# Moving the second layer's split input and merged branches two elements further in SBUF

## The chip, the cores and the metric

The kernel runs on one core of one Trainium2 chip. The metric is the device time of one launch in microseconds (us); lower is better. Times without a profile are medians over runs. A profile is one more execution, recorded by the hardware profiler.

## The reference

A two-layer encoder over 272 tokens (16 learned tokens in front of 256 real ones, numbered 0 to 271 below), with 2048 channels, in float32. Cut to what matters here:

```python
for i in range(2):
    h = rmsnorm(x, norm_mix[i])
    q, k, v, f, ga, gf = split(h @ w_in[i])                 # one projection of the normed input
    a = attention(rope(rmsnorm(q)), rope(rmsnorm(k)), v) @ w_attn_br[i]
    s = fft2(f).real @ w_four[i]
    merged = sigmoid(ga + b) * a + sigmoid(gf + b) * s
    x = x + merged @ w_out[i]
    up = rmsnorm(x, norm_ffn[i]) @ w_up[i]                  # 2048 -> 2 * 5632
    g = conv3(up[:, :5632]) * w + b                         # over tokens t-1, t, t+1
    x = x + (silu(g) * up[:, 5632:]) @ w_down[i]
return x[16:]                                               # the 16 learned tokens are dropped
```

Only tokens 16 to 271 are returned. So in the second layer most of the work is done for tokens 16 to 271 alone, or, where the convolution needs the token before, for tokens 14 to 271, which is 258 columns.

## The kernel before

Everything is stored with channels on the 128 partitions and tokens along a partition. Each float32 matrix product is made from numbers split in two parts of reduced precision, a high part H and a low part L, and three products are summed in PSUM: weight H by input H, weight H by input L, weight L by input H.

The weights stream from HBM in chunks of 512 KB (128 partitions by 4 KB) into four buffers `raw`, ScalarE casts a chunk to its high part `wh` (L242), VectorE subtracts to make the low part `wl` (L245), and TensorE uses the two as stationary operands. A planner writes out the whole sequence of chunks before the first instruction; loads and splits run two chunks ahead of the products, and the order in which TensorE takes its groups is written out by hand.

The function `group` is where nearly all products are made: for a pair of 128-channel outputs it goes over all chunks, and for each 128-channel slice of the input issues the three products, each with its own load of stationary weights:

```python
a, b = x
nc.tensor.matmul(o, h[:, c, sl], a, start=kt == 0, stop=False)         # L314
nc.tensor.matmul(o, h[:, c, sl], b, start=False, stop=False)           # L315
nc.tensor.matmul(o, lo[:, c, sl], a, start=False, stop=kt == nk - 1)   # L316
```

The input that streams through the array is one row of `T` = 272 tokens of a split tensor, 1,088 bytes of a partition, or a part of that row from token `lo` on. In the first layer `lo` is 0; in the second it is 14 for the queries, the gates, the branch and output projections and the gate half of the FFN, and `lo2` is 16 for the value half of the FFN.

The tensors that the change touches:

- `xHL` (L388 and the line below it) holds the normed input of the projections, as 16 slices of two rows each, H and L. It is written by `norm_split` (L458 and L459), in the first layer for the mixing part, at the end of that layer's output projections for its FFN, in the first layer's last `w_down` groups for the second layer, and at the end of the second layer's output projections for its FFN. It is read by all projections `f`, `k`, `v`, `q`, `ga`, `gf` and by both FFN halves `ug` and `uv`. In the second layer `uv` reads H and L of a slice with one product of two rows of 256 tokens (L310, 512 columns) and H again with the low weights (L311, 256 columns).
- `mHf` and `mLf`, in pool slots of `AHn` and `ALn` elements, hold the merged branches, 8 rows of 272 tokens each, written by ScalarE and VectorE after each attention branch group `a`, and read by the output projections `o`. The same slots serve for other tensors earlier in the layer: the attention weights `PH` and `PL`, the folded input and the channel transforms.
- The attention output `qH`, `qL`, read by the groups `a`, is not touched by the change.

The last 12 blocks of the second layer's FFN and the products of its `w_down` work the other way around: there the activations (`tH`, `tL`, `opnd`) are stationary and the split weights stream as 512 or 256 columns (L1291, L1356).

Addresses: a pool gives each tile a place that is a multiple of 32 bytes in the partition. In the built program `xHL` starts at byte 33,920, which is 530 times 64, and a row of 272 tokens is 17 times 64 bytes. So in the program before, every row of `xHL` starts on a multiple of 64 bytes, token 14 lies 56 bytes behind such a multiple, and token 16 lies on one. The second layer's `mH` and `mL` start 32 bytes behind a multiple of 64, and their token 14 lies 24 bytes behind one.

Of the kernel before, what the change touches and what calls it, by code (L numbers as in the profile page):

```python
# [10 lines left out]
F32 = mybir.dt.float32  # L11
F32R = mybir.dt.float32r
AF = mybir.ActivationFunctionType
# [3 lines left out]
P = 128  # L17
# [3 lines left out]
T = NM + SEQ  # L21
DEPTH = 2
KT = D // P
# [11 lines left out]
FF_SPLIT = (24, 20)  # L35
# [97 lines left out]
def encoder_kernel(ctx, tc, xT, params, consts, bmat, cfold, csign, w_fl, w_f64c, w_in, w_abr, w_four, w_f64, w_out, w_up, w_down, w_dn, w_dt, out):  # L133
    nc = tc.nc
# [48 lines left out]
    t, done = 0, 0  # L183
# [174 lines left out]
    def first_groups(pss):  # L358
        assert order[st["grp"]][0] == (0, "f01")
        st["grp"] += 1  # L360
        ps = [psum.tile([P, 512], F32, tag="mm", name=f"ps_f01_{m}") for m in range(2 * MG)]
        pss += [ps[:MG], ps[MG:]]
        for kt in range(KT // CW * 2 * CW):
            q, j, c = kt // (2 * CW), kt // CW % 2, kt % CW
            k = CW * q + c
            if c == 0:
                if kt == 0:
                    norm_split(0, P_NM)
                    split_w(0, 0, 1)
                    norm_split(1, P_NM)  # L370
                    split_w(0, 1, 2)
                    norm_split(2, P_NM)
                    split_w(0, 2, 4)
                    norm_split(3, P_NM)
                    st["fetch"] = 1
                h, lo = splits.pop(st["next"])
                st["next"] += 1
            for m in range(MG):
                sl = slice(m * P, (m + 1) * P)
                o = ps[MG * j + m][:, :T]  # L380
                a, b = xH[:, k, :], xL[:, k, :]
                nc.tensor.matmul(o, h[:, c, sl], a, start=k == 0, stop=False)
                nc.tensor.matmul(o, h[:, c, sl], b, start=False, stop=False)
                nc.tensor.matmul(o, lo[:, c, sl], a, start=False, stop=k == KT - 1)
            if j == 1 and CW * (q + 1) + c < KT:
                norm_split(CW * (q + 1) + c, P_NM)
            if c in (0, 2):
                advance(st["next"] + (1 if c == 0 else 2))  # L388
                pump(len(chunks))
            if kt == 0:  # L390
                tc.keep_in_program_order(nc.sync.dma_start(XT[:, 12:16, :], xT[:, 12:16, :]))
                tc.keep_in_program_order(nc.sync.dma_start(cst[:, C_MASK:C_CC], consts[:, C_MASK:C_CC]))
            step()


    XT = per.tile([P, KT, T], F32, name="XT")
    xHL = per.tile([P, KT, 2, T], F32R, name="xHL")
    xH, xL = xHL[:, :, 0, :], xHL[:, :, 1, :]
    prm = per.tile([P, P_N], F32, name="prm")
    cst = per.tile([P, C_N], F32, name="cst")  # L400
    ones = per.tile([P, P], F32, name="ones")
# [53 lines left out]

    def norm_split(m, goff):
        gc = prm[:, goff + m:goff + m + 1]
        nc.scalar.activation(xH[:, m, :], XT[:, m, :], AF.Copy, scale=gc)  # L458
        nc.vector.scalar_tensor_tensor(xL[:, m, :], XT[:, m, :], gc, xH[:, m, :].bitcast(F32),  # L459
                                       op0=ALU.mult, op1=ALU.subtract)  # L460

    def norm_sum(m):
# [75 lines left out]
        nc.vector.tensor_tensor(tok2, tok, tok, op=ALU.mult)  # L538
        holder["tok2"] = tok2

    xr = lambda lo: (lambda kt: (xH[:, kt, lo:T], xL[:, kt, lo:T]))
    slow[1] = weight_sums()

    for l in range(DEPTH):
# [6 lines left out]
        with tc.tile_pool(name=f"mix{l}", bufs=1) as mp:  # L551
            E = mp.tile([P, 4, 2, TH] if last else [P, NG, T], F32, tag="q1b" if last else "q1", name="E")
            e64 = mp.tile([2 * NG, TH], F32, tag="u", name="e64", bufs=2) if last else None
            AHn = 3 * 4 * T
            ALn = 2 * 4 * T
            o1 = []

            def o1_tiles():
# [422 lines left out]
            def attention(kv, rq):  # L981
# [6 lines left out]
                PHf = mp.tile([P, AHn], F32R, tag="aH", name="PH")  # L988
                PLf = mp.tile([P, ALn], F32R, tag="aL", name="PL")
                PH = PHf.rearrange("p (b h t) -> p b h t", b=3, h=4)  # L990
                PL = PLf.rearrange("p (b h t) -> p b h t", b=2, h=4)

                def scores(item):
                    if item is None:
# [124 lines left out]
            for half in range(2):  # L1119
                slow[2] = 0  # L1120
                mH = mL = None
                for kind, i in BRANCH_ORDER[half]:
                    j = i - 4 * half
                    if kind == "ga":
                        tha[i] = gate("ga", i)
                    elif kind == "gf":
                        w64s.append(split_w64(l, i))
                        thf[i] = gate("gf", i)
                    elif kind == "s":
                        def s_evac(m, ps, th=thf[i]):  # L1130
                            e, o = (mp.tile([P, TH], F32, tag=t, name=t) for t in ("se", "so"))
                            for a, p_ in ((e, ps[0]), (o, ps[1])):
                                nc.scalar.copy(a, p_[:, TH:2 * TH])
                                nc.vector.tensor_tensor(a, p_[:, :TH], a, op=ALU.add)
                            sp = mp.tile([P, T], F32, tag="sp", name="sp", bufs=2)
                            nc.vector.tensor_tensor(sp[:, 0:TH], e, o, op=ALU.add)
                            nc.vector.tensor_tensor(sp[:, TH:T], e[:, T - TH:0:-1], o[:, T - TH:0:-1], op=ALU.subtract)
                            t_ = th[:, m, lo:T]
                            nc.vector.scalar_tensor_tensor(t_, t_, 1.0, sp[:, lo:T], op0=ALU.add, op1=ALU.mult)

                        four_group((l, "s", i), fr, x64, w64s.pop(0), s_evac)
                    else:
                        if mH is None:
                            drain()
                            mHf = mp.tile([P, AHn], F32R, tag="aH", name="mH")
                            mLf = mp.tile([P, ALn], F32R, tag="aL", name="mL")
                            mH = mHf[:, :8 * T].rearrange("p (k t) -> p k t", k=8)
                            mL = mLf[:, :8 * T].rearrange("p (k t) -> p k t", k=8)
                        ps = group((l, "a", i), lambda kt: (qH[kt // 4][:, kt % 4, lo:T], qL[kt // 4][:, kt % 4, lo:T]), W)
                        for m in range(MG):  # L1150
                            k = 2 * j + m
                            t_, h_ = tha[i][:, m, lo:T], mH[:, k, lo:T]
                            nc.vector.scalar_tensor_tensor(t_, t_, 1.0, ps[m][:, :W], op0=ALU.add, op1=ALU.mult)
                            nc.vector.tensor_tensor(t_, t_, thf[i][:, m, lo:T], op=ALU.add)
                            nc.scalar.copy(h_, t_)
                            nc.vector.tensor_tensor(mL[:, k, lo:T], t_, h_.bitcast(F32), op=ALU.subtract)
                slow[2] = (18 if last else 24) if last or half else 0
                for mg in range(8):
                    ps = group((l, "o", half, mg), lambda kt: (mH[:, kt, lo:T], mL[:, kt, lo:T]), W)
                    for m in range(MG):  # L1160
                        mt = 2 * mg + m
                        nc.vector.scalar_tensor_tensor(XT[:, mt, lo:T], ps[m][:, :W], 0.5, XT[:, mt, lo:T], op0=ALU.mult, op1=ALU.add)
                        if half == 1:
                            norm_in(mt, P_NF + l * KT)


        with tc.tile_pool(name=f"ffn{l}", bufs=1) as fp:
# [25 lines left out]
            def split_to(h, low, v):  # L1193
                nc.scalar.copy(h, v)
                nc.vector.tensor_tensor(low, v, h.bitcast(F32), op=ALU.subtract)

            k0 = 0
            for c, n in enumerate(() if last else FF_SPLIT):
                gHL = fp.tile([P, FF_SPLIT[0], 2, T], F32R, tag="gHL", name="gHL")
                gH, gL = gHL[:, :, 0, :], gHL[:, :, 1, :]  # L1200
                for i in range(k0 // MG, (k0 + n) // MG):
                    cs = conv_gate(i)
                    ps = group((l, "uv", i), xr(0), T)
                    for m in range(MG):
                        j = 2 * i + m - k0
                        nc.vector.tensor_tensor(cs[m], cs[m], ps[m][:, :T], op=ALU.mult)
                        split_to(gH[:, j], gL[:, j], cs[m])
                for mg in range(8):
                    ps = group((l, "d", c, mg), lambda kt: (gH[:, kt], gL[:, kt]), T)
                    for m in range(MG):  # L1210
                        mt = 2 * mg + m
                        nc.vector.tensor_tensor(XT[:, mt], XT[:, mt], ps[m][:, :T], op=ALU.add)
                        if c == len(FF_SPLIT) - 1:
                            norm_in(mt, P_NM + (l + 1) * KT)
                k0 += n
# [3 lines left out]
            if last:  # L1219
# [92 lines left out]
                for i in range(FT // MG):  # L1312
                    cs = conv_gate(i)
                    if i == 0:
                        for s_ in range(2):
                            nc.vector.tensor_scalar(sgn[:, s_], hold["tok"][:, 1:3], 1.0 - 2 * s_, None, op0=ALU.mult)
                    ps = group((l, "uv", i), lambda kt: (xHL[:, kt, :, lo2:T],), W2)
                    for m in range(MG):
                        j = 2 * i + m
                        cv = cs[m][:, lo2:T]  # L1320
# [111 lines left out]
```

## Time and profile before

| | |
|---|---|
| median of 3 runs | 2552.93 us (2552.89 to 2554.19) |
| the profiled execution's own time | 2552.66 us |
| its span, first to last instruction | 2550.8 us |
| TensorE busy | 2541.1 us, 19184 matmuls |
| weight loads | 2467.0 us |
| VectorE busy | 1775.1 us |
| ScalarE busy | 1270.8 us |
| moved by DMA | 591.45 MB, mean 232 GB/s |

The profile names a group of instructions by its line in the kernel, its engine, its operation, and what it writes and reads (out<-in) with shapes; then come the count, the busy time in us and the mean duration of one in ns, and after the bar the idle time of the engine just before them. A matmul's duration runs until its last column has left the array, so durations of successive matmuls overlap: their sum is more than the time that passes, and differences of durations between shapes show what columns cost.

### The profile page before, as it was taken

The page shows a single profiled execution, that of the slowest core. Times are in us where ns is not written, and L with a number is a line of the kernel's source. Part 1 is how long each engine was busy: PE and PEld are TensorE (multiplying, and loading weights), DVE is VectorE, ACT ScalarE, POOL GpSimd, SP SyncE. Part 2 cuts the span into 40 slices and gives each one's busy share as a digit, 9 for nine tenths or more (in the row PEclk, how much of TensorE's full clock was granted, in tenths as well). Part 3 has the DMA queues.
Part 4 walks back from the last instruction along what each step waited for, and adds up shares of the span by engine and source line. Part 5 has one row for each costly group of instructions (what it writes and reads, how often), then busy time and mean ns, then how long its engine had stood idle before and what let it go on. Part 6 is the DMA issues. An engine that isn't in the chain of part 4 may idle for free.

```text
span 2550.8 us, 47527 instructions
## 1 busy us (share of the span) xinstructions
PE 2541.1 (100%) x19184; PEld 2467.0 (97%) x19184; DVE 1775.1 (70%) x2804; ACT 1270.8 (50%) x1820; POOL 78.4 (3%) x169
## 2 busy tenths in 40 slices
PE   9999999999999999999999999999999999999999
PEld 8999999999999999999999999999999999988887
DVE  7687866776666556666559877666756666788886
ACT  5455434554444334444445555444644444566665
POOL 0000000000000000000000000000000000000000
PEclk9999999999999999999999999999999999999999
DMA  6545555689898988888775546765878555787887
GB/s 237 165 155 160 192 181 180 221 249 298 273 280 286 281 298 275 289 272 281 236 228 193 180 142 194 240 211 193 258 251 253 189 183 187 226 265 262 259 303 247
DMA packets 158731, 591.45 MB, mean 232 GB/s; under 512 B 18080, under 2 KB 23328, under 8 KB 158000
## 3 DMA queue, kind: packets, MB, share of 16 engines
q1 hardware_dynamic: 147344, 519.19, 60.5%
q0 software_dynamic: 9728, 67.11, 10.8%
q8 instruction: 150, 2.46, 0.4%
q10 hardware_dynamic: 1440, 2.13, 0.2%
q14 instruction: 69, 0.57, 0.1%
HBM read 566.70 MB, written 85.98 MB: 256 GB/s over the span
## 4 chain that ended last, share of the span: by engine, by line
PE 98%; DMA 1%; DVE 1%; issue 0%; ACT 0%; SPq 0%; POOL 0%; ACTq 0%
PE ps_ug L315 7%; PE ps_ug L316 7%; PE ps_ug L314 7%; PE ps_uv L310 6%; PE ps_p L1291 6%; PE ps_d L315 3%; PE ps_uv L314 3%; PE ps_uv L315 3%; PE ps_d L314 3%; PE ps_uv L316 3%; PE ps_d L316 3%; PE ps_uv L311 3%; PE ps_t L1356 3%; PE ps_o L315 2%; PE ps_gf L314 2%; PE ps_gf L315 2%
## 5 line engine op out<-in xcount | busy, mean ns | idle before, releaser
L245 DVE TENSOR_TENSOR wl<-raw,wh 128x1024 fp32r<-128x1024 f32 (+1 forms) x901 | 1090.9, 1218 | 640.1 <-ACT wh L242 629.2
L242 ACT CAST wh<-raw 128x1024 fp32r<-128x1024 f32 (+1 forms) x901 | 937.5, 1044 | 968.1 <-PE ps_ug L315 195.1
L315 PE MATMUL ps_ug<-xHL,wh 128*128 128x272 f32 (+1 forms) x1408 | 402.3, 286 | 0.0
L314 PE MATMUL ps_ug<-xHL,wh 128*128 128x272 f32 (+1 forms) x1408 | 402.3, 286 | 0.0
L316 PE MATMUL ps_ug<-xHL,wl 128*128 128x272 f32 (+1 forms) x1408 | 401.5, 285 | 0.0
L314 PEld LDWEIGHTS ps_ug<-xHL,wh 128*128 128x128 f32 x1408 | 265.2, 188 | 1.7
L315 PEld LDWEIGHTS ps_ug<-xHL,wh 128*128 128x128 f32 x1408 | 265.5, 189 | 1.0
L316 PEld LDWEIGHTS ps_ug<-xHL,wl 128*128 128x128 f32 x1408 | 264.9, 188 | 0.1
L310 PE MATMUL ps_uv<-xHL,wh 128*128 128x512 f32 x704 | 248.9, 395 | 0.0
L315 PE MATMUL ps_uv<-xHL,wh 128*128 128x272 f32 x704 | 203.1, 288 | 0.0
L314 PE MATMUL ps_uv<-xHL,wh 128*128 128x272 f32 x704 | 202.9, 288 | 0.0
L314 PE MATMUL ps_d<-gHL,wh 128*128 128x272 f32 x704 | 202.9, 288 | 0.0
L315 PE MATMUL ps_d<-gHL,wh 128*128 128x272 f32 x704 | 202.9, 288 | 0.0
L316 PE MATMUL ps_uv<-xHL,wl 128*128 128x272 f32 x704 | 202.8, 288 | 0.0
L316 PE MATMUL ps_d<-gHL,wl 128*128 128x272 f32 x704 | 202.1, 287 | 0.0
L311 PE MATMUL ps_uv<-xHL,wl 128*128 128x256 f32 x704 | 197.6, 281 | 0.0
L310 PEld LDWEIGHTS ps_uv<-xHL,wh 128*128 128x128 f32 x704 | 132.4, 188 | 29.8
L314 PE MATMUL ps_ga<-xHL,wh 128*128 128x272 f32 (+1 forms) x512 | 148.1, 289 | 0.0
L314 PE MATMUL ps_gf<-xHL,wh 128*128 128x272 f32 (+1 forms) x512 | 147.2, 288 | 0.0
L315 PE MATMUL ps_o<-mL,wh 128*128 128x272 f32 (+1 forms) x512 | 146.5, 286 | 0.0
L315 PE MATMUL ps_gf<-xHL,wh 128*128 128x272 f32 (+1 forms) x512 | 146.3, 286 | 0.0
L316 PE MATMUL ps_ga<-xHL,wl 128*128 128x272 f32 (+1 forms) x512 | 146.2, 285 | 0.0
(355 smaller groups left out, 5825.9 us busy)
## 6 DMA issues: line engine op xcount, KB each, us to landing
raw<-in_w_up SPq DMA_DIRECT2D x352, 512.0 KB, 4.6
raw<-in_w_in SPq DMA_DIRECT2D x191, 512.0 KB, 3.6
raw<-in_w_down SPq DMA_DIRECT2D x88, 512.0 KB, 4.9
raw<-in_w_out SPq DMA_DIRECT2D x64, 512.0 KB, 3.7
raw<-ft SPq DMA_DIRECT2D x64, 512.0 KB, 4.6
ft<-in_w_dn POOLq DMA_DIRECT2D x24, 1024.0 KB, 12.2
raw<-in_w_dn SPq DMA_DIRECT2D x48, 512.0 KB, 4.5
raw<-in_w_abr SPq DMA_DIRECT2D x32, 512.0 KB, 3.5
```

The source lines that it names most:

```text
L242: nc.scalar.copy(h[:, a:b], r[:, a:b])
L245: nc.vector.tensor_tensor(lo[:, a:b], r[:, a:b], h[:, a:b].bitcast(F32), op=ALU.subtract)
L310: nc.tensor.matmul(o2, h[:, c, sl], ab, start=kt == 0, stop=False)
L311: nc.tensor.matmul(o, lo[:, c, sl], ab[:, 0, :], start=False, stop=kt == nk - 1)
L314: nc.tensor.matmul(o, h[:, c, sl], a, start=kt == 0, stop=False)
L315: nc.tensor.matmul(o, h[:, c, sl], b, start=False, stop=False)
L316: nc.tensor.matmul(o, lo[:, c, sl], a, start=False, stop=kt == nk - 1)
L1291: nc.tensor.matmul(ps[h], x, w[:, 512 * h:512 * h + 512], start=i == 0 and w is wh and x is a, stop=i == NQ - 1 and w is wl)
L1356: nc.tensor.matmul(ps[r][:, :c1 - c0], x[:, kt, tk], w[:, q, c0:c1], start=kt == 0 and x is tH and w is wh, stop=kt == NT - 1 and w is wl)
```

## The change

`xHL` is allocated two elements (8 bytes) longer as a flat tile, and `view.x`, `view.h` and `view.l` are views into it that start at element 0 or, after `shift_x(2)`, at element 2. The switch is made in the first layer's FFN just before the last set of `w_down` groups, whose results are normed and split for the second layer. From there on all reads and writes of the split input lie two elements further. The merged branches of the second layer lie two elements further in their slots too, and the slot `aL` is two elements longer for that.

```diff
-    xHL = per.tile([P, KT, 2, T], F32R, name="xHL")
-    xH, xL = xHL[:, :, 0, :], xHL[:, :, 1, :]
+    xf = per.tile([P, KT * 2 * T + 2], F32R, name="xHL")
+
+    class view:
+        pass
+
+    def shift_x(n):
+        view.x = xf[:, n:n + KT * 2 * T].rearrange("p (k r t) -> p k r t", k=KT, r=2)
+        view.h, view.l = view.x[:, :, 0, :], view.x[:, :, 1, :]
+
+    shift_x(0)
...
-    xr = lambda lo: (lambda kt: (xH[:, kt, lo:T], xL[:, kt, lo:T]))
+    xr = lambda lo: (lambda kt: (view.h[:, kt, lo:T], view.l[:, kt, lo:T]))
...
-            ALn = 2 * 4 * T
+            ALn = 2 * 4 * T + 2
...
-                            mH = mHf[:, :8 * T].rearrange("p (k t) -> p k t", k=8)
-                            mL = mLf[:, :8 * T].rearrange("p (k t) -> p k t", k=8)
+                            off = 2 if last else 0
+                            mH = mHf[:, off:off + 8 * T].rearrange("p (k t) -> p k t", k=8)
+                            mL = mLf[:, off:off + 8 * T].rearrange("p (k t) -> p k t", k=8)
...
+                if c == len(FF_SPLIT) - 1:
+                    shift_x(2)
...
-                    ps = group((l, "uv", i), lambda kt: (xHL[:, kt, :, lo2:T],), W2)
+                    ps = group((l, "uv", i), lambda kt: (view.x[:, kt, :, lo2:T],), W2)
```

In the built program of the changed kernel all instructions stand in the same order on every engine as before. Addresses differ in two ways:

- Those the edit names. Token 14 of `xHL`, `mH` and `mL` in the second layer lies on a multiple of 64 bytes, token 16 (read by `uv`) and token 0 (read by `k` and `v`) 8 bytes behind one.
- Those behind it. Since places are multiples of 32 bytes, the 8 bytes at the end of `xHL` move every tile placed after it by 32 bytes, and the 8 bytes of `aL` move what lies behind that slot by 32 more. The weight buffers `raw`, `wh` and `wl`, which started on multiples of 64, start 32 bytes behind one; so do `gHL` (the first layer's input of `w_down`), the first layer's `mH`, `mL` and `qH`, and `tH`, `tL` and `opnd`.

More of the change, by code (lines that the diff above doesn't have):

```diff
@@ L380, in first_groups @@
                 o = ps[MG * j + m][:, :T]
-                a, b = xH[:, k, :], xL[:, k, :]
+                a, b = view.h[:, k, :], view.l[:, k, :]
                 nc.tensor.matmul(o, h[:, c, sl], a, start=k == 0, stop=False)
@@ L457, in norm_split @@
         gc = prm[:, goff + m:goff + m + 1]
-        nc.scalar.activation(xH[:, m, :], XT[:, m, :], AF.Copy, scale=gc)
-        nc.vector.scalar_tensor_tensor(xL[:, m, :], XT[:, m, :], gc, xH[:, m, :].bitcast(F32),
+        nc.scalar.activation(view.h[:, m, :], XT[:, m, :], AF.Copy, scale=gc)
+        nc.vector.scalar_tensor_tensor(view.l[:, m, :], XT[:, m, :], gc, view.h[:, m, :].bitcast(F32),
                                        op0=ALU.mult, op1=ALU.subtract)
@@ L990, in attention @@
                 PH = PHf.rearrange("p (b h t) -> p b h t", b=3, h=4)
-                PL = PLf.rearrange("p (b h t) -> p b h t", b=2, h=4)
+                PL = PLf[:, :2 * 4 * T].rearrange("p (b h t) -> p b h t", b=2, h=4)
                 def scores(item):
```

## The prediction

> **What bounds the kernel now.** I read the profile's page first: span, busy times, the granted clock and the chain that ended last.
>
> ```profile
> span 2550.8 us, 47527 instructions
> PE 2541.1 (100%) x19184; PEld 2467.0 (97%) x19184; DVE 1775.1 (70%) x2804; ACT 1270.8 (50%) x1820; POOL 78.4 (3%) x169
> ...
> PEclk9999999999999999999999999999999999999999
> ...
> PE 98%; DMA 1%; DVE 1%; issue 0%; ACT 0%; SPq 0%; POOL 0%; ACTq 0%
> ```
>
> TensorE is busy for 2541.1 of 2550.8 us at a full clock, and 98% of the chain is TensorE. Next I read the waits of TensorE, whose longest line is the start of the kernel:
>
> ```profile
> PE ps_f L382 <- ACT wh L242: 5.2, 3, 4.5
> ```
>
> So nothing that VectorE, ScalarE or a DMA does is late anywhere else, and the order of instructions does not change. The change can act through one thing only: how long TensorE takes for a matmul whose operand lies at another address. Times 19184 matmuls, half a nanosecond is 9.6 us, so small prices count. About 0.2%, 5.1 us, is what a measurement of this kernel can tell from no change.
>
> That matmuls stand end to end is seen in stretches of one group each: a gate group and a value group of the second layer's FFN, and a long stretch of first-layer `w_down` groups. The columns are the stretch, its length, TensorE's busy time with its count, the clock, the DMA share and GB/s.
>
> ```profile
> 830.00:930.00 100.00, 100.00 (x799) 1.00 0.93 289
> ...
> 1961.42:1972.95 11.53, 11.53 (x98) 1.00 0.57 186
> 1972.95:1984.16 11.21, 11.21 (x66) 1.00 0.56 188
> ```
>
> Two or so of each count only reach into the stretch. The gate group has 16 slices by 2 outputs by 3 products, 96 matmuls of 258 columns in 11.53 us, 120.1 ns each. The `w_down` stretch has about 797 of 272 columns in 100 us, 125.5 ns each. The value group has 32 pairs of 512 and 256 columns in 11.21 us, 350 ns a pair. Now the rows by line and shape, where the second number behind the bar is the mean of one in ns:
>
> ```profile
> L310 PE MATMUL ps_uv<-xHL,wh 128*128 128x512 f32 x704 | 248.9, 395 | 0.0
> L314 PE MATMUL ps_ug<-xHL,wh 128*128 128x272 f32 x704 | 203.2, 289 | 0.0
> ...
> L315 PE MATMUL ps_ug<-xHL,wh 128*128 128x272 f32 x704 | 203.1, 288 | 0.0
> ...
> L316 PE MATMUL ps_ug<-xHL,wl 128*128 128x272 f32 x704 | 202.7, 288 | 0.0
> ...
> L315 PE MATMUL ps_ug<-xHL,wh 128*128 128x258 f32 x704 | 199.2, 283 | 0.0
> L314 PE MATMUL ps_ug<-xHL,wh 128*128 128x258 f32 x704 | 199.1, 283 | 0.0
> L316 PE MATMUL ps_ug<-xHL,wl 128*128 128x258 f32 x704 | 198.8, 283 | 0.0
> L311 PE MATMUL ps_uv<-xHL,wl 128*128 128x256 f32 x704 | 197.6, 281 | 0.0
> ```
>
> Per matmul that is 609.0/2112 = 288.4 ns for 272 columns, 597.1/2112 = 282.7 for 258 and 197.6/704 = 280.7 for 256. The first and the last start on a multiple of 64 bytes, the middle one 56 bytes behind one. A straight line between the two aligned shapes has (288.4 - 280.7)/16 = 0.48 ns a column and gives 281.6 at 258. The 258 columns take 1.1 ns more than that. This small excess is all that an aligned token 14 can be seen to win.
>
> **The change part by part.**
>
> *Products that come to lie on 64 bytes.* In the second layer `ug`, `ga`, `gf`, `q` and `o` have three lines each of the counts above and here:
>
> ```profile
> L314 PE MATMUL ps_ga<-xHL,wh 128*128 128x258 f32 x256 | 73.2, 286 | 0.0
> L314 PE MATMUL ps_gf<-xHL,wh 128*128 128x258 f32 x256 | 72.9, 285 | 0.0
> ...
> L314 PE MATMUL ps_o<-mH,wh 128*128 128x258 f32 x256 | 72.4, 283 | 0.0
> ...
> L314 PE MATMUL ps_q<-xHL,wh 128*128 128x258 f32 x128 | 37.6, 294 | 0.0
> ```
>
> That makes 3 x (704 + 256 + 256 + 256 + 128) = 4800 matmuls. At 1.1 ns each they win 5.3 us. The least is nothing: the excess can belong to the number 258 and not to its place. The most comes from the lowest row of 256 columns, in the tail, 6.7 us for 24 or 279.2 ns:
>
> ```profile
> L1356 PE MATMUL ps_t<-wh,tH 128*128 128x512 f32 x84 | 33.2, 395 | 0.0
> ...
> L1356 PE MATMUL ps_t<-wh,tH 128*128 128x256 f32 x24 | 6.7, 280 | 0.0
> ```
>
> Two columns more give 280.1, so 2.6 ns below the present 282.7, or 12.5 us. I take 1.1, since its rows are of the same tensor and the same stage.
>
> *Products that leave 64 bytes for 8 bytes behind.* The value half reads three rows per slice and output, two in L310 and one in L311: 704 x 3 = 2112 rows. `k` and `v` add 3 x 64 matmuls each:
>
> ```profile
> L314 PE MATMUL ps_k<-xHL,wh 128*128 128x272 f32 x64 | 19.0, 298 | 0.0
> ...
> L314 PE MATMUL ps_v<-xHL,wh 128*128 128x272 f32 x64 | 19.0, 296 | 0.0
> ```
>
> These rows hold both layers, so half of them, 192 matmuls, are moved. No row shows a long run at 8 bytes. With the same 1.1 ns a row, 2304 rows lose 2.5 us. The bounds are nothing and four columns' worth a row (a row that begins inside a group of four columns touches one group more): 4 x 0.48 = 1.9 ns, 4.4 us.
>
> *Streamed operands that move by 32 bytes.* This part is not in the edit's words. The first layer's `d` (2112), `o` (768) and two thirds of its `a` (256), 3136 matmuls, and the tail, where the split weights stream:
>
> ```profile
> L314 PE MATMUL ps_d<-gHL,wh 128*128 128x272 f32 x704 | 202.9, 288 | 0.0
> ...
> L314 PE MATMUL ps_o<-mH,wh 128*128 128x272 f32 x256 | 73.5, 287 | 0.0
> ...
> L1291 PE MATMUL ps_p<-wh,opnd 128*128 128x512 f32 x448 | 121.1, 391 | 0.0
> ...
> L1291 PE MATMUL ps_p<-wl,opnd 128*128 128x512 f32 x224 | 69.4, 391 | 0.4 <-DVE wl L245 0.4
> ```
>
> That is 672 in `ps_p` and 3 x (84 + 24) = 324 in `ps_t`, 996 in all. The trace has rows of operands that start 32 bytes behind a multiple of 64: the first layer's `a`, where `qL` of L315 does and `qH` of the other two does not, and the scores, where `kH` and `kL` do.
>
> ```profile
> L314 PE MATMUL ps_a<-q,wh 128*128 128x272 f32 x128 | 37.1, 290 | 0.0
> L315 PE MATMUL ps_a<-q,wh 128*128 128x272 f32 x128 | 37.0, 289 | 0.0
> L316 PE MATMUL ps_a<-q,wl 128*128 128x272 f32 x128 | 36.9, 289 | 0.0
> ...
> L1003 PE MATMUL ps_s<-kL,q 128*128 128x272 f32 x32 | 9.2, 287 | 0.0
> ```
>
> `a` takes 111.0/384 = 289.1 ns, 0.7 more than `ug`; were the one product in three the whole cause, it would pay 2.1 ns. The scores pay nothing, but come in short runs. I take 0.7: 2.2 us for the first layer and 0.7 us for the tail, with nothing and 2.1 ns as ends (6.6 and 2.1 us). What moves between 0 and 32 both ways (the Fourier part, two tensors of the attention) cancels or is under 100 matmuls.
>
> *Weights that move by 32 bytes.* All stationary `wh` and `wl` move. The token products `ps_fb` have three of four weights on 64 bytes in the first layer and 32 behind in the second; they are short, so that the weight load sets their pace. The stretches of the two layers:
>
> ```profile
> 72.00:90.50 18.50, 4.03 (x32) 1.00 0.44 143
> 1429.00:1441.00 12.00, 4.05 (x32) 1.00 0.42 121
> ```
>
> 0.02 us over 24 moved loads is under 1 ns, where the load is the bound. In a long product it lies under the stream. I take nothing for it.
>
> *VectorE, ScalarE and DMA* write and read at the new places. They wait on nobody new, and the 5.2 us above is all that TensorE waits for a weight anywhere, so their cover is the two chunks of lead; a price of 5% on a VectorE split would still leave it idle a quarter of the time at its mean of 70%.
>
> **Sum.** Against the profiled execution's 2552.66 us: -5.3 + 2.5 + 2.2 + 0.7 = +0.1 us, so 2552.8; the median of runs lies 0.3 us above that execution, so 2553.
>
> **The rivals.**
>
> *The aligned products win more.* If 258 columns fall to the tail's pace, they win 12.5 us, and if a start 32 bytes behind costs nothing, as in the scores, only the 2.5 us of the value half is lost: -10.0 us, 2543. For it: the gate group's 120.1 ns is well above the 2 columns' distance from the tail's 256. Against it: 256 columns of `xHL` itself take 280.7, not 279.2. It decides from a win of 1.6 ns with 32 bytes free.
>
> *Slower: the 32 bytes behind.* The place is the first layer's `w_down` and output projections and the tail. At 2.1 ns a matmul they lose 6.6 + 2.1 = 8.7 us, the value half 2.5; with half of the gain left (-2.7) the sum is +8.5 us, 2561, and with none of it 2564. For it: `a` with its 289.1. Against it: the scores with 287.5. With the full gain it passes +5.1 us at (5.1 + 5.3 - 2.5)/4132 = 1.9 ns, with none at 0.6.
>
> *Places count only through the groups of four columns touched.* 258 columns from byte 56 touch 65 groups, and from byte 64 also 65, so nothing is won; the value rows and `k`, `v` touch one more, +4.4 us, and 32 bytes are a whole number of groups, so nothing else moves: 2557. The Trainium skill, page "SBUF — State Buffer", section "Specifications (TRN2)", has this rule: lines of 16 bytes, and each cross to a new line pays. By that rule the change cannot win. The rows here agree in that 282.7 lies above the line through 256 and 272, as a 65th group would have it (0.96 ns for two columns more); they do not show a price for a start.
>
> *Nothing depends on the place*, so that the aligned token 14 does not do what it is for: 2553, the same as the sum.
>
> **How the numbers follow.** The sum with its terms near the values taken has 0.27, four-column groups 0.10 and no dependence 0.05; all three lie within 0.2%: 0.42. The larger win has 0.25. The 32 bytes have 0.33, since the nearest row, that of `a`, has such a price, and since any small price on weights under a long product, of which there are over ten thousand, would add to it. The range takes in most of the win (to -9) and the loss with none of the gain: 2544 to 2564.
>
> **What would show it.** In the profile after, the 258-column rows of `ug`, `ga`, `gf` and `o` should stand near 281.6 ns and a gate group near 11.42 us; `uv` near 397 and 282; `d` near 289; `a` of the second layer, which keeps its places 24 bytes behind, at its present mean. TensorE must still wait for nobody. Wrong would be: a 258-column row unchanged, a row of `ug` or `uv` of the first layer (same stream, moved weights only) that is slower, or a wait for `wh` or `wl` in a `w_down` group, where the DMA share is already 0.93.

## The result: 0.18% slower

| | before | after |
|---|---|---|
| median, 16 runs each | 2553.78 us (2552.54 to 2556.60) | 2558.34 us (2557.11 to 2560.71) |
| span of the profiled execution | 2550.8 us | 2555.8 us |

The ratio is 1.0018, 95% interval 1.0011 to 1.0025. The two profiles differ by 5.0 us in span. The page of the changed kernel:

```profile
span 2555.8 us, 47529 instructions
...
PE 2546.2 (100%) x19184; PEld 2469.3 (97%) x19184; DVE 1774.9 (69%) x2804; ACT 1273.0 (50%) x1820; POOL 78.7 (3%) x169
```

TensorE is busy 5.1 us longer with the same 19184 matmuls. Its waits are no longer than before, 5.6 us in all, and nearly all of that is the start of the kernel:

```profile
PE ps_f L382 <- ACT wh L242: 4.8, 2, 4.5
PE ps_fa L615 <- DVE E L594: 0.5, 1, 0.5
PE ps_p L1302 <- DVE wl L245: 0.3, 1, 0.3
```

So all of it is in the duration of matmuls. The rows by line and shape after the change, in the order of the view, the costliest first:

```profile
L310 PE MATMUL ps_uv<-xHL,wh 128*128 128x512 f32 x704 | 252.0, 398 | 0.0
...
L315 PE MATMUL ps_ug<-xHL,wh 128*128 128x272 f32 x704 | 203.2, 289 | 0.0
L315 PE MATMUL ps_d<-gHL,wh 128*128 128x272 f32 x704 | 202.9, 288 | 0.0
L314 PE MATMUL ps_d<-gHL,wh 128*128 128x272 f32 x704 | 202.9, 288 | 0.0
...
L314 PE MATMUL ps_ug<-xHL,wh 128*128 128x272 f32 x704 | 202.6, 288 | 0.0
L316 PE MATMUL ps_ug<-xHL,wl 128*128 128x272 f32 x704 | 202.6, 288 | 0.0
...
L316 PE MATMUL ps_ug<-xHL,wl 128*128 128x258 f32 x704 | 199.7, 284 | 0.0
L314 PE MATMUL ps_ug<-xHL,wh 128*128 128x258 f32 x704 | 199.7, 284 | 0.0
L315 PE MATMUL ps_ug<-xHL,wh 128*128 128x258 f32 x704 | 199.3, 283 | 0.0
L311 PE MATMUL ps_uv<-xHL,wl 128*128 128x256 f32 x704 | 198.2, 282 | 0.0
```

Beside the rows of before: `uv` +3.1 and +0.6 us; the aligned 258 columns of `ug` 598.7 against 597.1, so **+1.6 us where a gain was forecast**; the first layer's `ug`, whose input did not move, 608.4 against 609.0, so 0.6 us faster, and the first layer's `uv` likewise, 608.2 against 608.8; `d`, whose input moved by 32 bytes along with its weights, unchanged to a tenth.

The same is seen without the overlap of durations in stretches cut from the first matmul of a group to the first of the next. Three are used from here on: a gate group of the second layer (`ug`, 96 matmuls), the value group behind it (`uv`, 64), and a gate group of the first layer (96). Ahead of the tail's products, all groups of one kind in one profile (third to fourteenth block of the second layer, third to tenth of the first) agree within 0.015 us, so one row stands for all. Before:

```profile
2052.38:2063.91 11.53, 11.53 (x98) 1.00 0.56 183
2063.91:2075.12 11.21, 11.21 (x66) 1.00 0.58 188
725.16:737.21 12.05, 12.05 (x98) 1.00 0.82 288
```

and after:

```profile
2054.54:2066.11 11.57, 11.57 (x98) 1.00 0.56 183
2066.11:2077.47 11.36, 11.36 (x66) 1.00 0.57 186
724.65:736.67 12.03, 12.03 (x98) 1.00 0.83 298
```

22 value groups of +0.15 us make 3.3 us, the largest part; 22 gate groups of +0.045 us (11.526 and 11.571 between the first matmuls) make 1.0; 44 first-layer groups of `ug` and `uv` at -0.027 us (12.053 and 12.026) give 1.2 back. Most of the rest of the 5.0 us is in rows of the second layer that moved too: those of `ga` and `gf` stand 0.9 us higher than before, those of `k` and `v` 0.5.

### The profile page after: what moved, and what is told of

Its sections match the earlier page's. It is cut to its first block, busy times and chain, and to the rows that moved or that the text cites. A ratio compares the mean times of both kernels' runs of the same rounds, so it can differ in the third digit from the quotient of the medians.

```text
span 2555.8 us, 47529 instructions
## 1 busy us (share of the span) xinstructions
PE 2546.2 (100%) x19184; PEld 2469.3 (97%) x19184; DVE 1774.9 (69%) x2804; ACT 1273.0 (50%) x1820; POOL 78.7 (3%) x169
## 4 chain that ended last, share of the span: by engine, by line
PE 99%; DVE 1%; DMA 0%; ACT 0%; issue 0%; SPq 0%; ACTq 0%
PE ps_ug L315 7%; PE ps_ug L316 7%; PE ps_ug L314 7%; PE ps_uv L310 6%; PE ps_p L1302 6%; PE ps_d L315 3%; PE ps_uv L315 3%; PE ps_d L314 3%; PE ps_uv L316 3%; PE ps_d L316 3%; PE ps_uv L314 3%; PE ps_uv L311 3%; PE ps_t L1367 3%; PE ps_o L315 2%; PE ps_gf L314 2%; PE ps_gf L316 2%
## 5 line engine op out<-in xcount | busy, mean ns | idle before, releaser
L314 PE MATMUL ps_gf<-xHL,wh 128*128 128x272 f32 (+1 forms) x512 | 147.4, 288 | 0.0
L316 PE MATMUL ps_gf<-xHL,wl 128*128 128x272 f32 (+1 forms) x512 | 146.5, 286 | 0.0
```

## The experiments

The change has two halves: the shift, and the 32 bytes by which everything behind moves. Three theories were set against each other. A: a stream pays for the groups of four columns (16 bytes) that it touches. B: a stream pays for a start off 64 bytes. C: what counts is the distance in the address between the stream and the weights that are loaded.

**The shift alone** (`e1`): both tensors are made 64 bytes longer, so that what lies behind keeps its place relative to 64 bytes.

```diff
-    xf = per.tile([P, KT * 2 * T + 2], F32R, name="xHL")
+    xf = per.tile([P, KT * 2 * T + 16], F32R, name="xHL")
-            ALn = 2 * 4 * T + 2
+            ALn = 2 * 4 * T + 16
```

> The changed kernel with both tensors padded by 64 bytes instead of 8, so that the two-element shift stays and every tile behind keeps its old place relative to 64 bytes (weights on 64 again). Theory A, the streamed operand pays for each group of four columns that it touches and nothing else: the first layer is as before (ug and uv there 125.5 ns a matmul), the second layer's uv still loses about 3.3 us and k, v 0.4 us, ug, ga and gf go back to what they were before (120 ns, the 2.4 us that they lost in the changed kernel come back), so 2553 + 4 = 2557 us. Theory B, every streamed start off 64 bytes costs about 1 ns: ug, ga, gf, q, o win about 5 us, uv loses 2.5, so 2551. Theory C, what counts is where the stream lies relative to the weights that are being loaded: ug and ga with both on 64 behave like the first layer, 119 to 119.7 ns, and uv stays slower; 2553 to 2556.

Measured 2558.60 us, ratio 1.0016 (1.0008 to 1.0025). The three stretches:

```profile
2055.31:2066.89 11.58, 11.58 (x98) 1.00 0.56 183
2066.89:2078.23 11.35, 11.35 (x66) 1.00 0.56 186
724.76:736.82 12.06, 12.06 (x98) 1.00 0.81 274
```

The loss is the shift's: `uv` pays as in the changed kernel, and `ug`, with token 14 and the weights both on 64 bytes, is slower than before too. B is out for `ug`; A has `uv` right but not `ug`.

**The 32 bytes alone** (`e2`): `shift_x(2)` becomes `shift_x(0)` and `off` 0, the lengths stay as in the change.

> The other half alone: both tensors 8 bytes longer as in the change, so that everything behind moves by 32 bytes, but nothing is shifted: token 14 stays at 56 bytes, token 16 at 0. Theory A: only the 32 bytes of the weights can act; the first layer's ug and uv at 125.3 ns as in the changed kernel (1.2 us won there), the second layer's uv back at 350 ns a pair; 2552 to 2553. Theory B: the 3136 first-layer products and the tail that start 32 bytes off lose, 2554 to 2557. Theory C: uv and ug of the second layer, whose stream now lies 32 bytes from the weights, move as the first layer's do, by about -0.3 ns a matmul, 2551 to 2553.

Measured 2550.15 us, ratio 0.9982 (0.9973 to 0.9991): faster than the kernel before.

```profile
2049.43:2060.92 11.48, 11.48 (x98) 1.00 0.56 184
2060.92:2072.13 11.21, 11.21 (x66) 1.00 0.59 189
724.78:736.80 12.03, 12.03 (x98) 1.00 0.83 288
```

The first layer's gate group is at the changed kernel's 12.03, and the second layer's, which nobody shifted here, is below before's 11.53. So the unnamed half of the change was its good half.

**A shift of four** (`e3`: as `e1`, with `shift_x(4)` and `off` 0).

> The input shifted by four elements instead of two with the weights kept on 64 bytes and the merged branches not shifted: token 16 (uv) lies 16 bytes behind a multiple of 64, token 14 (ug, ga, gf, q) 8 bytes behind. Theory A: 256 columns from byte 16 touch 64 groups as before, so uv and k, v cost what they cost before (350 ns a pair), and 258 columns touch 65 as before: 2553 us, no change. Theory B: uv starts off 64 bytes just as in the changed kernel and loses the same 3 us or so, ug does not win: 2556. Theory C: no forecast beyond B's range.

Measured 2551.97 us, ratio 0.9987 (0.9978 to 0.9996).

```profile
2053.68:2065.18 11.50, 11.50 (x98) 1.00 0.56 184
2065.18:2076.31 11.14, 11.14 (x66) 1.00 0.61 190
726.78:738.84 12.06, 12.06 (x98) 1.00 0.81 290
```

`uv` starts off 64 bytes, on 16, and is faster than before. B is out for `uv` as well. A forecast no loss, and had no reason for a gain.

**Two more tokens** (`e4`: the kernel before with `lo = 12`).

> The kernel before with the second layer starting at token 12 instead of 14: 260 columns from byte 48 in place of 258 from byte 56, two tokens more are computed in the projections, gates, branches and the gate half of the FFN. Theory A: 260 columns from byte 48 touch 65 groups, as 258 from byte 56 do, so ug, ga, gf, o, q stay at 120.0 ns and the time at 2553. If columns are paid one by one at 0.46 ns, 4800 matmuls and the 384 of the attention branch lose 0.9 ns each, 4.8 us: 2558. Theory B: a start at 48 costs the same as one at 56, so the columns' 0.9 ns come on top: 2558.

Measured 2553.14 us, ratio 0.9994 (0.9986 to 1.0003), the same.

```profile
2053.54:2065.10 11.55, 11.55 (x98) 1.00 0.56 183
2065.10:2076.32 11.22, 11.22 (x66) 1.00 0.61 188
```

Two more columns in each of 4800 matmuls, which also start 8 bytes earlier, cost 0.02 us in a gate group of 96, or 0.3 ns a matmul, and nothing that shows in the whole. This spoke for A.

**A shift of five** (`f1`), made to hit A: 258 columns now touch 66 groups.

> As the run with a shift of four (weights on 64, merged branches not shifted), but five elements: 258 columns start 12 bytes behind a multiple of 16 and so hold 1 + 256 + 1 columns, 66 groups of four instead of 65; 256 columns start 4 bytes behind one, 65 groups instead of 64. Theory A: ug, ga, gf and q (4032 matmuls) pay a whole group, 1.85 ns each or 7.4 us, on the kernel before, and uv, k, v about 3.4 us: 2565 us. Theory B, a price for any start off 64 bytes: ug stays as before (its start was off before), uv loses 3 us as in the changed kernel: 2557. Theory C: as B.

Measured 2558.90 us, ratio 1.0020 (1.0011 to 1.0029).

```profile
2054.53:2066.06 11.53, 11.53 (x98) 1.00 0.57 183
2066.06:2077.53 11.47, 11.47 (x66) 1.00 0.55 184
```

`ug` with a 66th group takes what it took before. A falls for 258 columns. `uv` from 4 bytes behind 16 pays 0.25 us a group, more than from 8 bytes behind (0.14), with the same 65 groups a row, so A has the order of its cost wrong too.

**A shift of eight** (`f2`, lengths as in `e1`): the stream moves by 32 bytes and the weights by 64, where in `e2` the stream stays and the weights move by 32.

> Eight elements (32 bytes), weights on 64, merged branches not shifted: token 16 lies 32 bytes behind a multiple of 64, token 14 24 bytes. Theory A: 64 and 65 groups as before, no change in uv or ug: 2553. Theory B: uv loses 3 us. Theory C, the distance of stream and weights modulo 64 counts and 32 is the better one: uv, k and v come out as with the weights moved instead (247.0 us for all of uv, k and v as before), and ug likewise (253.9 us against 254.9): 2552.

Measured 2552.19 us, ratio 0.9992 (0.9983 to 1.0001).

```profile
2052.65:2064.14 11.48, 11.48 (x98) 1.00 0.58 184
2064.14:2075.34 11.21, 11.21 (x66) 1.00 0.59 189
726.38:738.44 12.06, 12.06 (x98) 1.00 0.77 270
```

The second layer's groups are those of `e2` to the hundredth, though both operands lie elsewhere. Only how far one moved against the other is the same.

**Everything 32 bytes further together** (`f3`: an unused tile ahead of the input in the kernel before, and `ALn` eight elements longer).

```diff
+    per.tile([P, 8], F32, name="gap")
     xHL = per.tile([P, KT, 2, T], F32R, name="xHL")
```

> The kernel before with an unused 32-byte tile ahead of the input, so that input, weights and all that follows move by 32 bytes together and nothing is shifted inside. Theory C, only the distance between stream and weights counts: the first layer's ug and uv are back at 265.7 and 265.2 us (125.5 ns), the second layer's ug at 254.9: 2553, no change. If weights 32 bytes behind 64 were faster by themselves, ug and uv of the first layer stay at 265.1 and 264.6 and the whole is 2550.

Measured 2553.77 us, ratio 0.9997 (0.9988 to 1.0007).

```profile
2052.17:2063.70 11.53, 11.53 (x98) 1.00 0.56 183
2063.70:2074.91 11.21, 11.21 (x66) 1.00 0.55 188
725.23:737.28 12.05, 12.05 (x98) 1.00 0.86 300
```

All three stretches are those of the kernel before. C holds: with both moved by 32 bytes the absolute places do not count, the distance does.

**Which partner** (`g3`: an unused 32-byte tile between the raw weight buffers and the split ones, in the kernel before). There is one execution, so only the stretches are read.

> The kernel before with an empty 32-byte tile between the raw weight buffers and the split ones: raw stays on 64 bytes, the split weights wh and wl and all behind them move by 32. If the partner of the stream is the weights that TensorE loads, every group comes out as with the 32 bytes before raw: ug and uv of the first layer 265.1 and 264.6 us, ug of the second 253.9. If it is what ScalarE and VectorE read or the DMA writes (raw), they stay at 265.7, 265.2 and 254.9.

```profile
2052.48:2063.97 11.48, 11.48 (x98) 1.00 0.55 184
2063.97:2075.18 11.21, 11.21 (x66) 1.00 0.60 189
726.59:738.62 12.03, 12.03 (x98) 1.00 0.83 285
```

As with everything behind the input moved. So the partner is not `raw`. It is `wh` and `wl`, or a tile behind them, since those moved as well; `g1` and `g2` below rule out the tiles of the FFN.

TensorE loads `wh` and `wl`, but ScalarE and VectorE also write them meanwhile, and a collision with these writes would be a rival. The start times in the traces speak against it. From one matmul's start to the next takes 226 ns at one place in a value group of the kernel before and 239 at another, for the same 512 columns, and at each place nearly the same in every group. Where a place was passed both while one of the two engines worked and while neither did, the two differ by 0.12 ns or less in the mean, in the second layer's gate groups and value groups of every run (in `e1`, where two patterns alternate, within each pattern). TensorE itself reads nothing but the input and the weights in these groups, so its own loads are the partner that is left. No run tests them alone.

**Adding gains.** Three versions were to add up what had been won. The first (`f4`) joins `e2` and `e3`: the 32 bytes and a shift of four.

> The two changes that won, together: everything behind the input moved by 32 bytes, and the second layer's input shifted by four elements so that uv starts on 16 bytes. If their gains add: -2.9 us of span from the 32 bytes, -1.7 us in uv, at most -0.5 us in ug beyond that, so 2549 us. Theory A: no more than the 32 bytes' gain from the groups' side, 2550. Theory C: uv now lies 16 bytes from the weights modulo 64 on the other side, with no forecast better than 2549 to 2553.

Measured 2553.50 us, ratio 0.9999 (0.9990 to 1.0008).

```profile
2052.04:2063.65 11.60, 11.60 (x98) 1.00 0.56 182
2063.65:2074.80 11.15, 11.15 (x66) 1.00 0.61 187
```

The gains do not add: at this distance, the input moved by 16 bytes and the weights by 32, `ug` is at its slowest, 11.60.

The next two (`g1` with a shift of twelve, `g2` of sixteen) move the weights by 96 bytes and put unused 32-byte tiles ahead of the pools of the first layer and of both FFNs.

> From what has been measured, theory C alone: the distance of the streamed operand from the weights modulo 64 bytes sets the pace. Weights 32 bytes behind 64; the second layer's input shifted by twelve elements, so that uv is at distance 16 (the best one seen, -1.7 us) and ug, ga, gf at 8 (-0.6, -0.2, -0.2); the first layer's streams all at distance 32, with an empty 32-byte tile ahead of its pools, so that d and o gain as ug and uv did (0.27 ns a matmul: -0.6 and -0.2 us on top of -1.2); the tail's stream at 32 from its stationary operands, unknown. Sum -4.5 us: 2549.5 where the kernel before has 2554. If the pace depends on absolute places, d and o stay at 265.1 and 96.4 us.

> As g1, but shifted by sixteen elements: uv at distance 32 (-0.2 us), ug, ga, gf at 24 (-1.0, -0.4, -0.4), the rest as in g1. Theory C: 253.9 us for ug, 247.0 for uv, d and o -0.8 us together, sum -4.0 us: 2550, as the run with the 32 bytes only or 1 us less.

Measured 2555.09 us, ratio 1.0004 (0.9995 to 1.0013), and 2555.75 us, ratio 1.0007 (0.9998 to 1.0016): both forecasts of the whole were missed. In `g1`:

```profile
2052.43:2063.93 11.50, 11.50 (x98) 1.00 0.59 184
2063.93:2075.06 11.14, 11.14 (x66) 1.00 0.58 190
726.69:738.76 12.07, 12.07 (x98) 1.00 0.90 299
```

The second layer's groups came as forecast, to the hundredth those of `e3`, which has the same distance. (The FFN's own tiles lie 32 bytes further from input and weights here than in `e3`, and in `g2` than in `e2`, without an effect on these groups.) Two things did not come as forecast. The first layer's gate group is slower, 12.07, not 12.03: weights 96 bytes further are not the same as 32, so the pattern does not repeat at 64 bytes, and theory C was wrong in its modulus. For the same reason `e1`, with its weights 64 bytes further, was the shift alone only up to a small rest: its first-layer group takes 12.06, not 12.05. And the tail's streams, moved away from their stationary operands, lost:

```profile
L1305 PE MATMUL ps_p<-wh,opnd 128*128 128x512 f32 x448 | 123.0, 395 | 0.0
...
L1305 PE MATMUL ps_p<-wl,opnd 128*128 128x512 f32 x224 | 70.5, 396 | 0.3 <-DVE wl L245 0.3
```

3.0 us more than before in these two rows. `g2` shares the 12.07 and the tail's loss, and has 11.48 and 11.21 in the second layer.

**The best version** (`h1`): the weights move by 64 bytes, the first layer's input by 32, the second's by 16, the first layer's other streams by 96; the tail keeps its distance.

```diff
-    xf = per.tile([P, KT * 2 * T + 2], F32R, name="xHL")
+    xf = per.tile([P, KT * 2 * T + 16], F32R, name="xHL")
-    shift_x(0)
+    shift_x(8)
-            ALn = 2 * 4 * T + 2
+            ALn = 2 * 4 * T + 16
-                            off = 2 if last else 0
+                            off = 0
-                    shift_x(2)
+                    shift_x(4)
...
+            if not last:
+                mp.tile([P, 8], F32, name="gap")
...
+            if not last:
+                fp.tile([P, 8], F32, name="gap")
```

> Every group at the best distance from the weights that a run has shown, as theory C would have it (distances as moved against the kernel before: minus how far the weights moved, plus how far the stream moved): the weights move by 64 bytes, the first layer's input by 32 (distance -32, ug and uv -1.2 us together), the second layer's by 16 (distance -48: uv -1.7, ug -0.6, ga and gf -0.4), the first layer's gHL, mH and mL by 96 (distance +32: d -0.4, o -0.2), the tail with the weights (no change). Sum -4.5 us, so 2549 to 2550 where the kernel before has 2553.5 to 2554; ratio 0.998 to 0.9985. If absolute places count, the first layer's ug, whose start now lies 32 bytes behind 64, stays at 265.7 us.

Measured 2547.99 us, ratio 0.9977 (0.9967 to 0.9987).

```profile
2049.67:2061.17 11.50, 11.50 (x98) 1.00 0.58 184
2061.17:2072.30 11.14, 11.14 (x66) 1.00 0.59 190
724.19:736.22 12.03, 12.03 (x98) 1.00 0.82 285
```

Every stretch is where its distance had put it in an earlier run. The span is 4.4 us below before's, where 4.5 were forecast, and the time is the lowest measured, though its interval overlaps that of `e2`. The first layer's input starts 32 bytes behind 64 here and is still at 12.03.

Put by distance (how far the stream moved less how far the weights moved, in bytes), the second layer's groups are:

| distance | kernels | gate group, us | value group, us |
|---|---|---|---|
| 0 | before, `f3` | 11.53 | 11.21 |
| -16 | `f4` | 11.60 | 11.15 |
| -24 | the change | 11.57 | 11.36 |
| -32 | `e2`, `f2`, `g2`, `g3` | 11.48 | 11.21 |
| -44 | `f1` | 11.53 | 11.47 |
| -48 | `e3`, `g1`, `h1` | 11.50 | 11.14 |
| -56 | `e1` | 11.58 | 11.35 |

The value group is slow exactly where the distance is no multiple of 16 bytes. The weights were only moved by multiples of 32, so these are also the kernels whose token 16 does not start on 16 bytes, and the runs do not tell the two apart. The gate group, whose 258 columns begin 8 bytes ahead of the value group's, follows no such rule: its slowest and its fastest place are 16 bytes apart.

## Why the prediction was right, and where it was not

The time, 4.6 us above before, lies in the range, within 0.2% as the likeliest case had it. That it lies so near is partly luck. The sum of +0.1 us missed by 4.5 us, nearly all of the 5.1 us that 0.2% allows, and its terms were off in both directions: without the 2.9 us for streams that move by 32 bytes, which did not come, it would have missed by 7.4.

- **"Products that come to lie on 64 bytes": this step failed.** It took the 1.1 ns by which 258 columns lie above the line through 256 and 272 as a price of the start, -5.3 us. The rows of `ug` give +1.6 us, and no run shows a gain from token 14 on 64 bytes (11.57 and 11.58 against 11.53, where the prediction named 11.42). With `ga`, `gf`, `q` and `o` the rows of this term come to +2.3 us. The excess is no price of a start: at 56, 24, 8, 12 and 0 bytes behind 64 the same 258 columns gave 11.53, 11.48, 11.50, 11.53 and 11.58, and in `f4` the same 8 bytes gave 11.60. It had its lower bound at nothing and should have reached below.
- **The value half: right in sign, too small.** 2.5 us were taken, and the two rows of `uv` give 3.7, with `k` and `v` 4.2. The upper bound, four columns a row (4.4 us with `k` and `v`), was the better value. The Trainium skill's rule on lines of 16 bytes ("SBUF — State Buffer", section "Specifications (TRN2)") fits the value half, in that starts on 16 bytes are fast (11.14 to 11.21 us a group) and others slow (11.35 to 11.47); it does not fit the 258 columns, where a 66th group cost nothing (11.53 us in `f1` as before).
- **Streams that move by 32 bytes: nothing, where 2.9 us were taken.** `d` stands at 607.9 us in its three lines before and after. The 0.7 ns read off the first layer's `a` was taken for a price of the place; `f3` shows that a place 32 bytes behind 64 costs nothing when the weights go along, and here they did.
- **Weights that move by 32 bytes: -1.2 us, where nothing was taken.** The bound came from `ps_fb`, whose pace the prediction put down to the weight load, and its stretches stayed as they were (4.03 and 4.04 us after the change). The long products, in which it took the load to be hidden, were where the move counted, in the other direction than the rival of the 32 bytes feared.
- **The rivals.** The larger win and the loss by 32 bytes in the first layer did not come. The groups-of-four rival named 2557, the nearest time, for a reason that holds for `uv` alone.
- **Nothing late, no waits** and the unchanged order held.

That a term could depend on the distance between two operands was in none of the cases. The trace of before may have had a hint of it in the first layer's `a`, whose `qL` started 32 bytes behind a multiple of 64 where `qH` and the weights did not; it was read as a matter of one operand's place. In the changed kernel `qH`, `qL` and the weights all start 32 bytes behind one, and the rows of `a` have lost 0.3 us. That fits a distance that counts, but no run tests it on `a`:

```profile
L314 PE MATMUL ps_a<-q,wh 128*128 128x272 f32 x128 | 37.0, 289 | 0.0
L316 PE MATMUL ps_a<-q,wl 128*128 128x272 f32 x128 | 36.9, 288 | 0.0
L315 PE MATMUL ps_a<-q,wh 128*128 128x272 f32 x128 | 36.8, 288 | 0.0
```

## What to carry to other kernels

When TensorE is the bound and its matmuls stand end to end, an edit that lengthens a tile by a few bytes changes the place of all that is allocated behind it, and the places of stream and stationary operand relative to each other were worth 0.2% either way here. Check the memory map for what an edit moves beside what it names, and test the two halves apart, by padding to the old alignment and by padding without the edit. Start streamed rows on 16 bytes, as paid for the 256 columns here, and measure the rest.

## What the runs showed of the hardware

- The pace of a long run of matmuls of one shape followed the distance between the streamed operand and the weights: for each distance of the table that several kernels have, their groups agree to 0.01 us in 11 (four kernels at -32 bytes, three at -48), and moving both together by 32 bytes changed nothing.
- ScalarE and VectorE at work beside it made no difference to that pace: 0.12 ns or less in the mean, at the same place in a group.
- The pattern is not periodic in 64 bytes: the first layer's gate group takes 12.05 us at 0, 12.03 with the weights 32 bytes further, 12.06 with 64 and 12.07 with 96. The unused tile ahead of the first layer's pool is not the cause of the last: `h1` has it too and stays at 12.03.
- Two more columns were nearly free: 260 columns 11.55 us a group, 258 columns 11.53. Their start moved by 8 bytes as well, so the price of the columns alone is not shown.
- What makes the distance count (the reads of weights and stream meeting in SBUF, or something inside the array) was not tried and stays open.
